# Mask set-up, weight splits, load order and identity transposes at the start of a hybrid decoder block

## The chip, the cores and the metric

The kernel runs on one core of a Trainium2 chip. The core has a matrix engine (TensorE; PE in the profile, PEld for its weight loads), a vector engine (VectorE, DVE), a scalar engine (ScalarE, ACT), a general engine (GpSimd, POOL) and a queue engine (SyncE, SP). Each takes its instructions in the order in which they are queued; they meet through semaphores. Loads and stores are DMAs, issued from the queues of SP and ACT. The metric is the device time of one execution in microseconds.

## The reference

One decoder layer over 1024 tokens of width 1024, in fp32. What matters here is how it begins and what the masks are for:

```python
h = rms_norm(x, norm1_g[l]).astype(dt)
proj = h @ w_in[l]
(hq, hf, hi, hg, sq, sk, sv, fq, fk, fv, ff) = jnp.split(proj, offsets, axis=-1)
o_hg = hgrn2_mixer(hq, hf, hi, hg, lower_bounds[l], hg_norm_g[l])   # 4 heads, chunks of 64
o_sb = stick_breaking_attn(...)    # 6 heads
o_fox = forgetting_attn(...)       # 6 heads
x = x + concat([o_hg, o_sb, o_fox]) @ w_out[l]
h2 = rms_norm(x, norm2_g[l]).astype(dt)
x = x + jnp.square(jax.nn.relu(h2 @ w_ff1[l])) @ w_ff2[l]
```

Within a chunk of 64 tokens, the HGRN2 mixer needs the products of every pair of tokens in causal order. The kernel builds them level by level, with one 0/1 mask for each level.

## The kernel before

The tokens are eight tiles of 128 (t = 0 to 7), and the width 1024 is eight slices of 128 rows of weights (k = 0 to 7). To keep fp32 accuracy, every large product is made of three matmuls (`mm3`): each operand is split into a high part (a cast to fp32r, on ACT, line 124) and a low part (operand less high part, line 127), and the products high x high, low x high and high x low are accumulated.

The work is cut into units: six attention units `m0` to `m5`, each with one stick-breaking and one forgetting head, and two HGRN2 units `hg0` and `hg1`. `ORDER` begins with m0 and hg0. For each unit the kernel loads its columns of `w_in`, splits them (`w_steps`), projects all tokens (`proj_attn`, `proj_hg`) and runs its core (`attn`, `hgrn`). The projection of the next unit lies beside the core of the present one.

The start is the first norm together with the first unit's projection:

- `load_x(t)` (line 184) loads a tile of x in two halves of 512 columns, the first from SP's queue and the second from ACT's. `load_gain` (line 174) loads the norm's gain, broadcast to all partitions, from ACT's queue.
- `norm1(t)` calls `norm_to_T`: ACT squares both halves and sums them (line 148), DVE adds the two sums (line 150), `rstd_of` makes the reciprocal root from two ACT steps and four small DVE steps (lines 131 to 140), DVE scales both halves (line 153), and PE transposes the eight 128x128 blocks (line 156, `n1tp`) into PSUM buffers of the tag "z", of which there are three. `to_hT` then makes the high part on ACT (line 163, `hTh`) and the low part on DVE (line 164, `hTl`). The buffers of the squares, which the scaled rows then take, come from the tags ("e", "r", "zs")[t % 3], two of each of the first two: tiles 1, 4 and 7 use "r".
- The first unit's weights come in four pairs of row slices, called a to d. A slice has six segments of 64 columns and six further gate columns in a DMA of their own (lines 212 and 216). The high part (`whi`) is cast on ACT; the engine of the low part (`wlo`) is given by `LO`, one letter for each unit in `ORDER`: G is GpSimd, V is VectorE.
- `LOADS` gives the order in which loads are issued and in which norms and splits are written: a digit is a token tile, g the gain, a letter a to d a pair of weight slices. Once the four pairs are there and the tile number is above 2, one step of the projection follows each norm. A projection step of a token tile (`tok`, 390 columns) is 24 matmuls at lines 167 to 169 into a buffer `pj`; four token tiles can have their `pj` open at once (`P0`).

`hg_consts` makes seven masks for the HGRN2 units, one for each of six levels and one for the diagonal. Each is set to one by DVE in a scratch tile `lmf`, cut out by POOL (`affine_select`, lines 530, 533 and 544) and cast to int32 by DVE (lines 536 and 547). It is written with time 0.98, at the end of the first unit's projection. The scratch has two buffers of its own in the pool `small`. The tag "r" is used later by the scans of the stick-breaking core (`sbr`, line 404), by `hqk` and by `hon`.

The order on the engines isn't the order of the text alone: a planner takes the instructions by their place in the text as priority, and puts on each engine whatever its own estimate of times says is ready. It also hands out the buffers of a tag, each of which is free again when all who use its previous tile are done.

At the end, the feed-forward phase lays its buffers into the space of `small`'s neighbours by a table, `PLACES`, in which a tile `pad` fills what is not used.

Of the kernel before, what the change touches and what calls it, by code (L numbers as in the profile page):

```python
# [8 lines left out]
F32 = mybir.dt.float32  # L9
# [9 lines left out]
P = 128  # L19
# [7 lines left out]
LB_FLOOR = 1e-30  # L27
NEG = -1e30
ZMAX = 40.0
C = 64  # L30
NC_ = T // C
FOXH = 6
# [7 lines left out]
    "SPAN": [(0, 0), (0, -0.1), (0, 0), (-0.1, 0.05), (-0.1, 0), (-0.1, 0), (0.15, 0), (-0.05, 0)],  # L40
    "POW": [0.7, 1.1, 1.3, 1.3, 0.9, 1.2, 1, 1.5],
    "LOADS": "01g2a3b4cd567",
    "P0": "ddttdddd",
    "HI": "AAVAAAAA",
    "LO": "GVVGVGVG",
    "HPW": [0, 50, 200, 200, 200, 200, 200, 200],
    "EV": ["VA", "AA", "AA", "AA", "AA", "VA"],
    "SKEW": [2, 2, 2, 2, 2, 2],
# [10 lines left out]
def hybrid_block(ctx, tc, x, lb_logits, norm1_g, w_in, hg_norm_g, sb_q_g, sb_k_g, fox_q_g, fox_k_g,  # L59
                 fox_f_bias, w_out, norm2_g, w_ff1, w_ff2, out):  # L60
    nc = tc.nc
    V, S, G, PE = nc.vector, nc.scalar, nc.gpsimd, nc.tensor
# [3 lines left out]
    small = ctx.enter_context(tc.tile_pool(name="small", bufs=2))  # L66
    held = {}

    def pool(name, side=None, space=None):

        kw = dict(space=space) if space else dict(side=side)
        held[name] = ExitStack()
        return held[name].enter_context(tc.tile_pool(name=name, bufs=1, reuse_waits="tile", **kw))
# [10 lines left out]
    def big(tag, name, shape=None, dt=F32):  # L84
        home = sb_a if tag == "hT" else sb_w if tag in ("w", "raw", "zs", "cb", "hb", "xt") else sb_t
        return home.tile(shape or [P, SHAPE.get(tag, 512)], dt, tag=tag, name=name, bufs=BUFS[tag])

    def pt(tag, name, n=512, dt=F32):
        return ps.tile([P, n], dt, tag="ps_" + tag, name=name, bufs=PBUFS[tag])

    xf = x[0]
# [6 lines left out]

    ident = const.tile([P, P], F32, name="ident")
    make_identity(nc, ident)  # L100
    identb = const.tile([P, P], BF16, name="identb")
    V.tensor_copy(identb, ident)
    eps_t = const.tile([P, 1], F32, name="eps_t")
# [75 lines left out]
    X0 = {}  # L179

    def load_x(t):
        X0[t] = [big("pair", "x_t") for _ in range(2)]
        for c in range(2):
            (nc.sync if c == 0 else nc.scalar).dma_start(out=X0[t][c], in_=xf[t * P:(t + 1) * P, c * 512:(c + 1) * 512])

    def norm1(t):
        norm_to_T(X0.pop(t), g1b, to_hT, t, "n1")
# [160 lines left out]
    def attn(name):  # L348
# [23 lines left out]
        def qtile(h, i):  # L372
# [14 lines left out]
            for c, w in reversed(pcs):  # L387
# [7 lines left out]
                if sbk:  # L395
# [3 lines left out]
                    zs = big("zs", "sbz")[:, :w]  # L399
                    V.tensor_scalar(out=zs, in0=z, scalar1=st["r"][i // 4][:, i % 4, 0:1], scalar2=ZMAX, op0=ALU.mult, op1=ALU.min)  # L400
                    S.activation(e, zs, AF.Exp)
# [99 lines left out]
    def hg_consts():  # L501

        lbl = const.tile([P, 2], F32, name="lbl")
        nc.sync.dma_start(out=lbl, in_=lb_logits[0].rearrange("(j p) -> p j", p=P))
        lbt = const.tile([P, 2], F32, name="lbt")
        V.tensor_tensor(out=lbt, in0=lbl, in1=lbl, op=ALU.subtract)
        S.activation(lbt, lbt, AF.Exp)
        lbr = const.tile([P, 2], F32, name="lbr")
        V.reciprocal(lbr, lbt)
        V.tensor_tensor(out=lbt, in0=lbt, in1=lbr, op=ALU.mult)  # L510
        lb = const.tile([P, 2], F32, name="lb")
        V.tensor_tensor(out=lb, in0=lbt, in1=lbt, op=ALU.subtract)
        lb1 = const.tile([P, 2], F32, name="lb1")
        V.tensor_scalar(out=lb1, in0=lb, scalar1=-1.0, scalar2=1.0, op0=ALU.mult, op1=ALU.add)
        lbc = const.tile([P, 2], F32, name="lbc")
        V.tensor_scalar(out=lbc, in0=lb, scalar1=LB_FLOOR, scalar2=None, op0=ALU.max)
        S.activation(lbc, lbc, AF.Ln)
        lbcn = const.tile([P, 2], F32, name="lbcn")
        V.tensor_scalar(out=lbcn, in0=lbc, scalar1=-1.0, scalar2=None, op0=ALU.mult)


        def level_mask(n):

            f = small.tile([P, C], F32, name="lmf", bufs=2)
            V.memset(f, 1.0)
            nb = C // (2 * n)
            for h in range(2):
                fv = f[h * HD:(h + 1) * HD].rearrange("p (b e n) -> p b e n", e=2, n=n)

                G.affine_select(out=fv, in_=fv, pattern=[[-2 * n, nb], [0, 2], [0, n]], base=0, channel_multiplier=1,  # L530
                                compare_op=ALU.is_ge, fill=0.0)

                G.affine_select(out=fv, in_=fv, pattern=[[2 * n, nb], [0, 2], [0, n]], base=n - 1, channel_multiplier=-1,
                                compare_op=ALU.is_ge, fill=0.0)
            m = const.tile([P, C // 2], I32, name=f"lm{n}")
            V.tensor_copy(m.rearrange("p (b n) -> p b n", n=n), f.rearrange("p (b e n) -> p b e n", e=2, n=n)[:, :, 1, :])
            return m

        def diag_mask():
            f = small.tile([P, C], F32, name="lmf", bufs=2)  # L540
            V.memset(f, 1.0)
            for h in range(2):
                fh = f[h * HD:(h + 1) * HD]
                G.affine_select(out=fh, in_=fh, pattern=[[-1, C]], base=0, channel_multiplier=1,
                                compare_op=ALU.is_equal, fill=0.0)
            m = const.tile([P, C], I32, name="lm0")
            V.tensor_copy(m, f)
            return m

        heads = const.tile([P, 2], F32, name="heads")  # L550
        V.memset(heads, 0.0)
        for h in range(2):
            V.memset(heads[h * HD:(h + 1) * HD, h:h + 1], 1.0)
        lmask = {n: level_mask(n) for n in N_LEVELS}
        dmask = diag_mask()
        HGC.update(heads=heads, lb1=lb1, lbc=lbc, lbcn=lbcn, lmask=lmask, dmask=dmask)

# [316 lines left out]
    for o in CFG["LOADS"]:  # L874
        if o == "g":
            g1b = load_gain(norm1_g, "g1b", "hb")
        elif o in "abcd":
            loads["abcd".index(o)]()
        else:
            load_x(int(o))  # L880
# [237 lines left out]
    for q in range(NPAIR):  # L1118
        steps[q][3]()
        if AHEAD <= q + 2 < NPAIR:  # L1120
            for f in steps[q + 2][:3]:
# [9 lines left out]
    X = {}  # L1131
    U = [None] * 4

    PLACES = {"f_m": {"xo": (16, [P, 512]), "usum": (4, [P, 512]), "t1": (2, [P, 2, 512]), "ya": (3, [P, 2, 512]), "pad": (1, [P, 136 + 2048])},
              "f_hop": {"w2f": (1, [P, 2, D]), "yf": (2, [P, 2, 512]), "fof": (4, [P, 2, 512])},
              "f_h": {"w2raw": (4, [P, 2, D]), "fop": (2, [P, 2, 512]), "pad2": (1, [P, 1024])},
              "f_a": {"w2g": (1, [P, 2, D]), "fog": (14, [P, 2, 512])}}
    homes = {}
    for name, tags in PLACES.items():
        home = pool(name, "left")  # L1140
# [25 lines left out]
    for q0 in range(0, NPAIR, GM):  # L1166
        first, last = q0 == 0, q0 + GM == NPAIR
        qps = range(q0, q0 + GM, 2)
        B, t1 = {}, {}
# [61 lines left out]
        if first:  # L1231
            load_x(1, 1)
# [6 lines left out]
        if first:  # L1239
            load_x(0, 0)  # L1240
# [40 lines left out]
    held["pb"].close()  # L1281
    for name in reversed(PLACES):
        held[name].close()
# [27 lines left out]
```

## Time and profile before

| | us |
|---|---|
| median of three runs | 1349.1 |
| lowest and highest run | 1346.22 and 1351.35 |
| the profiled execution | 1347.27 |
| its span in the profile | 1345.5 |

The profile has a page with busy times and a trace that can be asked by stage, tile, line and engine. In a timeline, a row gives the start and the length in us, the engine, the line, the operation, the tile that is written and those that are read, the shape, how many alike are merged, and in brackets the idle time ahead of it with what ended it. A row of a group gives counts and shortest, median and longest duration in ns, and when the first and the last began. "SPq" and "ACTq" are the queues in which DMAs are issued. Matmuls overlap in the pipe, so their rows are longer than the distance from one to the next. The page's clock row gives the share of the full TensorE clock that was granted.

### The profile page before, as it was taken

How to read it: one execution, taken by the hardware profiler on the slowest of the kernel's cores; microseconds unless marked ns; L12 is line 12 of the kernel's file. 1: busy time of each engine (PE TensorE's matmuls, PEld its weight loads, DVE VectorE, ACT ScalarE, POOL GpSimd, SP SyncE). 2: the span in 40 equal slices, each digit the busy share in tenths (PEclk: the TensorE clock that was granted, in tenths of full speed). 3: DMA queues.
4: the chain of work that ended last, by engine and by line, in shares of the span. 5: the costliest groups of instructions: out<-in, count | busy, mean ns of one | idle time of the engine just before them, and what ended most of it. 6: DMA issues, size and time to landing. Idle time of an engine off the chain costs nothing.

```text
span 1345.5 us, 19762 instructions
## 1 busy us (share of the span) xinstructions
PE 1283.0 (95%) x7200; PEld 1063.1 (79%) x7200; DVE 985.8 (73%) x1844; ACT 727.0 (54%) x1557; POOL 90.3 (7%) x138
## 2 busy tenths in 40 slices
PE   4999889989999999999798999999999999999998
PEld 4978789878688988767586888888887788888887
DVE  6758798766768788867579766666666897786965
ACT  5658445877878457776446454455454433333330
POOL 7000021002110130000000000000000000000000
PEclk9999999989899989999898999999999999999999
DMA  8200220301203025524443434444445972634322
GB/s 231 46 17 18 62 58 18 92 16 54 49 17 79 17 57 177 183 64 125 149 152 107 164 126 164 164 130 145 149 163 175 391 247 94 218 96 153 113 79 94
DMA packets 129737, 156.57 MB, mean 116 GB/s; under 512 B 46684, under 2 KB 73308, under 8 KB 129640
## 3 DMA queue, kind: packets, MB, share of 16 engines
q1 hardware_dynamic: 104496, 109.14, 26.8%
q10 hardware_dynamic: 25144, 46.17, 9.6%
q8 instruction: 57, 0.93, 0.3%
q14 instruction: 40, 0.33, 0.1%
HBM read 108.07 MB, written 47.21 MB: 115 GB/s over the span
## 4 chain that ended last, share of the span: by engine, by line
PE 80%; DVE 10%; ACT 4%; DMA 4%; issue 2%; SPq 0%; ACTq 0%; DVEq 0%
PE pj L167 6%; PE pj L169 6%; PE pj L168 6%; PE av L465 3%; PE atp L446 2%; PE pc L1021 2%; PE pc L1022 2%; PE pc L1023 2%; PE pd L1021 2%; PE pd L1022 2%; PE pd L1023 2%; PE pc L1202 2%; PE pc L1200 2%; PE pc L1201 2%; PE pa L1023 2%; PE pa L1021 2%
## 5 line engine op out<-in xcount | busy, mean ns | idle before, releaser
L167 PE MATMUL pj<-whi,hTh 128*128 128x384 f32 (+2 forms) x512 | 172.2, 339 | 0.0
L169 PE MATMUL pj<-whi,hTl 128*128 128x384 f32 (+2 forms) x512 | 171.9, 336 | 0.0
L168 PE MATMUL pj<-wlo,hTh 128*128 128x384 f32 (+2 forms) x512 | 170.6, 334 | 0.5 <-DVE wlo L127 0.4
L124 ACT CAST fah<-ya 128x1024 fp32r<-128x1024 f32 x56 | 58.7, 1048 | 166.8 <-PE pd L1201 50.0
L167 PEld LDWEIGHTS pj<-whi,hTh 128*128 128x128 f32 x512 | 98.7, 193 | 3.6 <-issue 1.1
L168 PEld LDWEIGHTS pj<-wlo,hTh 128*128 128x128 f32 x512 | 98.5, 192 | 3.5 <-issue 1.3
L169 PEld LDWEIGHTS pj<-whi,hTl 128*128 128x128 f32 x512 | 98.4, 192 | 2.3 <-issue 1.5
L127 DVE TENSOR_TENSOR fal<-ya,fah 128x1024 fp32r<-128x1024 f32 x56 | 68.3, 1219 | 23.2 <-ACT fah L124 23.1
L465 PE MATMUL av<-at,vst 128*64 128x256 f32 x480 | 71.3, 384 | 6.3 <-DVE at L452 3.0
L450 ACT COPY at<-atp 128x128 f32<-128x128 f32 (+3 forms) x120 | 55.5, 475 | 20.5 <-PE atp L446 19.5
L465 PEld LDWEIGHTS av<-at,vst 128*64 128x64 f32 x480 | 38.3, 144 | 33.2 <-issue 8.4
L127 DVE TENSOR_TENSOR fbl<-w2raw,fbh 128x1024 fp32r<-128x1024 f32 x48 | 58.0, 1215 | 1.6 <-ACT fbh L124 1.6
L408 ACT ACTIVATE sbz<-sbz 128x128 f32<-128x128 f32 (+3 forms) x72 | 37.7, 525 | 37.8 <-DVE sbz L407 37.2
L400 DVE TENSOR_SCALAR sbz<-z,qnr 128x128 f32<-128x128 f32 (+3 forms) x72 | 42.5, 611 | 20.6 <-PE z L394 12.9
L167 PE MATMUL po<-woh,mTh 128*128 128x512 f32 x128 | 52.1, 409 | 4.5 <-DMA mTh<-mix_m 3.6
L124 ACT CAST fbh<-w2raw 128x1024 fp32r<-128x1024 f32 x48 | 50.0, 1047 | 8.1 <-DMA w2raw<-in_w_ff_dram 5.1
L391 PE MATMUL z<-kst,qj 128*128 128x512 f32 (+3 forms) x144 | 51.3, 384 | 2.8 <-ACT qj L368 2.8
L1201 PE MATMUL pa<-fbl,fah 128*128 128x512 f32 x128 | 50.3, 395 | 1.9 <-DVE fbl L127 1.8
L1200 PE MATMUL pd<-fbh,fah 128*128 128x512 f32 x128 | 49.5, 399 | 2.3 <-ACT fbh L124 2.3
L168 PE MATMUL po<-wol,mTh 128*128 128x512 f32 x128 | 51.1, 399 | 0.0
L392 PE MATMUL z<-kst,qj 128*128 128x512 f32 (+3 forms) x144 | 49.6, 370 | 1.5 <-DVE qj L369 1.4
L169 PE MATMUL po<-woh,mTl 128*128 128x512 f32 x128 | 50.6, 398 | 0.0
(349 smaller groups left out, 3626.3 us busy)
## 6 DMA issues: line engine op xcount, KB each, us to landing
w1raw<-in_w_ff_dram SPq DMA_DIRECT2D x32, 512.0 KB, 4.6
w2raw<-in_w_ff_dram SPq DMA_DIRECT2D x16, 1024.0 KB, 7.1
ya<-yd_s SPq DMA_DIRECT2D x32, 512.0 KB, 3.6
yd_s<-y ACTq DMA_DIRECT2D x48, 256.0 KB, 4.6
ya<-yd_a SPq DMA_DIRECT2D x24, 512.0 KB, 3.7
wraw<-in_w_in_dram SPq DMA_DIRECT2D x48, 192.0 KB, 3.0
mix_m<-ot ACTq DMA_DIRECT2D x10, 512.0 KB, 3.7
wraw<-in_w_in_dram SPq DMA_DIRECT2D x16, 256.0 KB, 3.6
```

The lines of the kernel that those rows point to most:

```text
L124: S.copy(hi, raw)
L127: lo_eng.tensor_tensor(out=lo, in0=raw, in1=hi, op=ALU.subtract)
L167: PE.matmul(o, lhsT=lh, rhs=rh, start=start, stop=False)
L168: PE.matmul(o, lhsT=lh, rhs=rl, start=False, stop=False)
L169: PE.matmul(o, lhsT=ll, rhs=rh, start=False, stop=stop)
L450: S.copy(dst, tv)
L465: PE.matmul(o[h * HD:(h + 1) * HD, c0:], lhsT=st["v"][j // 4][:, j % 4, h, :], rhs=at[h][j // 4][:, j % 4, c0:], start=(j == 0), stop=(j = ...
L1021: PE.matmul(o, lhsT=wh[:, k], rhs=bh[:, k], start=start and k == 0, stop=False, **kw)
L1022: PE.matmul(o, lhsT=wh[:, k], rhs=bl[:, k], start=False, stop=False, **kw)
L1023: PE.matmul(o, lhsT=wl[:, k], rhs=bh[:, k], start=False, stop=k == 3, **kw)
L1200: PE.matmul(o, lhsT=lh[:, ts], rhs=rh, start=start and q == q0, stop=False, **kw)
L1201: PE.matmul(o, lhsT=lh[:, ts], rhs=rl, start=False, stop=False, **kw)
```

## The change

- The scratch of the masks, `lmf`, moves from `small` to the tag "r", and `pad` grows by the 512 bytes for each partition that become free there.
- The low parts of the first unit's weights are made on DVE.
- `LOADS` becomes tile 0, the gain, a, tile 1, b, tile 2, c, tile 3, d, and then tiles 4 to 7. In the text, the splits of a pair now follow each of the first four norms, and the projection's first step follows norm 4 instead of norm 5.
- Both halves of each tile of x are issued from SP's queue, but for the second half of tile 0, which stays with ACT.
- Thirty transposes of the identity matrix are put on PE ahead of all else, into one PSUM buffer of the tag "z". Nothing reads their result.

```diff
+WARM = 30
...
-    "LOADS": "01g2a3b4cd567",
+    "LOADS": "0ga1b2c3d4567",
...
-    "LO": "GVVGVGVG",
+    "LO": "VVVGVGVG",
...
     ident = const.tile([P, P], F32, name="ident")
     make_identity(nc, ident)
+
+    warm = pt("z", "warm")
+    for i in range(WARM):
+        PE.transpose(out=warm[:, :P], in_=ident, identity=ident)
...
     def load_x(t):
         X0[t] = [big("pair", "x_t") for _ in range(2)]
         for c in range(2):
-            (nc.sync if c == 0 else nc.scalar).dma_start(out=X0[t][c], in_=xf[t * P:(t + 1) * P, c * 512:(c + 1) * 512])
+            (nc.scalar if t == 0 and c else nc.sync).dma_start(out=X0[t][c], in_=xf[t * P:(t + 1) * P, c * 512:(c + 1) * 512])
...
         def level_mask(n):
-            f = small.tile([P, C], F32, name="lmf", bufs=2)
+            f = big("r", "lmf", [P, C])
...
         def diag_mask():
-            f = small.tile([P, C], F32, name="lmf", bufs=2)
+            f = big("r", "lmf", [P, C])
...
-    PLACES = {"f_m": {..., "pad": (1, [P, 136 + 2048])},
+    PLACES = {"f_m": {..., "pad": (1, [P, 136 + 2176])},
```

More of the change, by code (lines that the diff above doesn't have):

```diff
@@ L1132, in hybrid_block @@
     U = [None] * 4
-    PLACES = {"f_m": {"xo": (16, [P, 512]), "usum": (4, [P, 512]), "t1": (2, [P, 2, 512]), "ya": (3, [P, 2, 512]), "pad": (1, [P, 136 + 2048])},
+    PLACES = {"f_m": {"xo": (16, [P, 512]), "usum": (4, [P, 512]), "t1": (2, [P, 2, 512]), "ya": (3, [P, 2, 512]), "pad": (1, [P, 136 + 2176])},
               "f_hop": {"w2f": (1, [P, 2, D]), "yf": (2, [P, 2, 512]), "fof": (4, [P, 2, 512])},
```

## The prediction

> **What bounds the kernel now.** I read the page's busy shares first, then the busy time by stage, then the first 64 us as a timeline, engine by engine.
>
> ```profile
> span 1345.5 us, 19762 instructions
> ...
> PE 1283.0 (95%) x7200; PEld 1063.1 (79%) x7200; DVE 985.8 (73%) x1844; ACT 727.0 (54%) x1557; POOL 90.3 (7%) x138
> ```
> ```profile
> 0.00:14.00 14.00, 0.00 (x0) 0.00 (x0) 4.84 (x28) 7.26 (x22) 12.14 (x35) 1.00 0.92 265
> 14.00:25.00 11.00, 7.06 (x27) 6.09 (x28) 9.94 (x23) 6.38 (x20) 6.78 (x10) 0.84 0.96 238
> 25.00:40.00 15.00, 15.00 (x95) 14.85 (x94) 13.50 (x45) 10.97 (x40) 5.97 (x9) 1.00 0.90 196
> 40.00:50.00 10.00, 10.00 (x66) 9.84 (x65) 9.20 (x25) 6.30 (x20) 0.57 (x1) 1.00 0.00 1
> ```
>
> PE is the bound: of 62.5 us in which it idles, 17.9 lie before 25 us (14.0, and 11.0 less 7.06), and from 25 to 50 it never stops. (Columns of a stage: length; busy time of PE, PEld, DVE, ACT, POOL; granted clock; DMA share; GB/s.) So the change is worth what it brings the unbroken PE work forward. That work, the first unit's projection, ends here:
>
> ```profile
> 63.03 0.34 PE L167 MATMUL pj<-whi,hTh 128*128 128x390 f32 x1
> ...
> 63.39 0.34 PE L169 MATMUL pj<-whi,hTl 128*128 128x390 f32 x1
> 63.57 0.40 PE L167 MATMUL pj<-hTh,whi 128*128 128x512 f32 x1
> ```
> ```profile
> 33.11 1.03 PE L156 MATMUL n1tp<-ident,n1sq 128*128 128x128 f32 x8
> 33.90 0.43 PE L168 MATMUL pj<-wlo,hTh 128*128 128x390 f32 x1
> ```
>
> A matmul starts every 0.18 us (three from 63.03 to 63.57), a transpose takes 0.11 (just under 0.9 us from the first of eight to the next in line, with the pipe's tail). The stage holds 8 token tiles x 24 matmuls x 0.178 = 34.2 us, 64 norm transposes x 0.11 = 7.0, and 8 more for keys and gates, 0.9: 42.1 us. It ends at 63.5, so it runs as if PE had started at **21.4 us** and never stopped. What held it off is on DVE:
>
> ```profile
> 7.96 0.10 DVE L150 TENSOR_TENSOR n1s<-n1ss 128x1 f32<-128x1 f32 x1
> ...
> 10.41 0.16 DVE L138 SCALAR_TENSOR_TENSOR n1t<-n1t,n1v 128x1 f32<-128x1 f32 x1
> 11.71 0.18 DVE L536 CAST lm<-lmf 128x32 int32<-128x32 f32 x1 [1.14 <-POOL lmf L533]
> 11.80 1.82 DVE L140 SCALAR_TENSOR_TENSOR n1r<-n1t,n1y 128x1 f32<-128x1 f32 x1
> ...
> 13.68 1.43 DVE L153 SCALAR_TENSOR_TENSOR n1sq<-x_t,n1r,g1b 128x512 f32<-128x512 f32 x2
> ...
> 15.72 4.32 DVE L153 SCALAR_TENSOR_TENSOR n1sq<-x_t,n1r,g1b 128x512 f32<-128x512 f32 x4
> ...
> 20.85 0.68 DVE L164 TENSOR_TENSOR hTl<-n1tp,hTh 128x512 fp32r<-128x512 f32 x1
> ```
> ```profile
> 31.34 1.41 DVE L153 SCALAR_TENSOR_TENSOR n1sq<-x_t,n1r,g1b 128x512 f32<-128x512 f32 x2
> ```
> ```profile
> 15.76 5.29 POOL L127 TENSOR_TENSOR wlo<-wraw,whi 128x384 fp32r<-128x384 f32 x6
> ```
>
> The first norm's sum and its 0.16 us steps stand in DVE's queue behind mask casts that wait for POOL, and where POOL splits weights, DVE's own operations stretch: 4.32 us for four scalings, against 1.41 for two at 31.34, when POOL is idle.
>
> **The change part by part.** *Masks.* They now take their scratch from the two "r" buffers, which the norm squares of tiles 1, 4 and 7 use ahead of them in program order, so they come behind the last norm. Tile 0 then meets no mask:
>
> ```profile
> 4.84 0.63 ACT L148 ACTIVATE n1sq<-x_t 128x512 f32<-128x512 f32 x1 [2.75 <-DMA x_t<-in_x_dram]
> ...
> 5.47 0.61 ACT L148 ACTIVATE n1sq<-x_t 128x512 f32<-128x512 f32 x1
> ...
> 9.80 0.29 ACT L131 ACTIVATE n1ln<-n1s,eps_t 128x1 f32<-128x1 f32 x1
> 10.00 0.19 ACT L133 ACTIVATE n1y<-n1ln 128x1 f32<-128x1 f32 x1
> ```
> ```profile
> L153 DVE SCALAR_TENSOR_TENSOR n1sq<-x_t,n1r,g1b x16: 737/748/1584, 13.7 to 44.0; 128x512 f32<-128x512 f32 x16
> L174 ACTq DMA_DIRECT2D g1b<-in_norm_g_dram x2: 453/453/453, 1.7 to 2.2; - x2
> ...
> DMA to landing us min/median/max: 5.6/6.0/6.3
> ```
>
> Both squares end at 6.2; five DVE steps of 0.16 and ACT's two (0.29, 0.19) give the scale at about 7.6. The gain row g1b lands 5.6 to 6.3 us after issue at 1.7 and 2.2, so at 7.3 and 8.5: scaling 7.6 to 9.2, first transpose at **8.4** instead of 14.60. *Loads.* All but one half of x goes to SP, so ACT loses seven issues (0.33 us each; one of them waited in ACT's order until 18.85) and SP issues 31 transfers before the constants: 15 halves of x and 16 pieces of weight.
>
> ```profile
> L184 SPq DMA_DIRECT2D x_t<-in_x_dram x8: 327/403/430, 0.8 to 18.6; - x8
> L184 ACTq DMA_DIRECT2D x_t<-in_x_dram x8: 334/334/445, 0.8 to 18.8; - x8
> ```
> ```profile
> L212 SPq DMA_DIRECT2D wraw<-in_w_in_dram x14: 378/434/560, 2.2 to 30.0; - x14
> L216 SPq DMA_DIRECT2D wraw<-in_w_in_dram x8: 339/542/681, 4.2 to 16.5; - x8
> ```
>
> That is 15 x 0.40 + 8 x (0.43 + 0.54) = 13.8 us of SP, less than the about 23 us that the same bytes take on DMA engines that are 0.92 to 0.96 busy: cost 0, unless SP waits, then up to 2 us on the last tiles, which nobody wants before 30 us. The order matters: the fourth pair of weight rows now has four token tiles ahead of it, not five, so 4.1 MB instead of 4.6; at 250 GB/s and from 1 us on it lands at 17 to 18. A token can't be finished before.
>
> *Splits on DVE.* Eight of 384 columns and eight of 6:
>
> ```profile
> L127 DVE TENSOR_TENSOR wlo<-wraw,whi x32: 533/552/694, 61.1 to 430.7; 128x384 fp32r<-128x384 f32 x24, 128x512 fp32r<-128x512 f32 x8
> ```
>
> 8 x (0.55 + 0.15) = 5.6 us more on DVE, 1.4 per pair of rows. Against that it is rid, before the last norm, of seven mask casts of 0.18, of 1.6 in the stretched L140 and of 1.5 in the four scalings (4.32 against 2 x 1.41): 4.4 us, about 1 less than comes. And now splits and norms share a queue. One step (a norm and a pair) is five small operations 0.8, scaling 1.41, hTl 1.37, pair 1.4: 5.0 us. Four steps from 7.0 end at 27; pairs are split at about 10.6, 15.6, 20.6 and 25.6, and the loads, by 18 us, are ahead of that.
>
> *PE under these.* One token against one pair is 6 matmuls, 1.07 us. By 17.5 there is work for two tiles' transposes (1.75) and four such pieces (4.3). From the third split, 19.7 on, more is ready than PE can do: the third tile's transposes 0.87, two pieces for old tokens, three for the new one, then the fourth split with eight. PE has done 6.9 us by 19.7, so it runs as if started at 19.7 - 6.9 = **12.8**. Bounds: 11.0 if the splits are put ahead of the scalings (all work of 18 us then done 1.8 earlier), 15.0 if each of four steps loses 0.5 us to DVE and ACT waiting for each other. Gain 21.4 - 12.8 = **8.6 us**, between 6.4 and 10.4.
>
> *Thirty transposes.* ident is ready at 1.65, long before x. They cost PE nothing while it is idle until 8.4; at 0.23 us (below) they end at 8.6, a delay of 0.2, and much less if the clock rises in between. What they can bring is the clock:
>
> ```profile
> 21.00:22.00 1.00, 0.41 (x2) 0.42 (x3) 1.00 (x3) 0.00 (x0) 0.05 (x1) 0.64 1.04 373
> 22.00:23.00 1.00, 1.00 (x6) 1.00 (x5) 0.97 (x4) 0.27 (x1) 0.00 (x0) 0.50 1.03 369
> ...
> 24.00:25.00 1.00, 1.00 (x5) 0.96 (x5) 0.24 (x3) 1.00 (x5) 0.00 (x0) 0.66 0.05 0
> ```
> ```profile
> 14.60 1.94 PE L156 MATMUL n1tp<-ident,n1sq 128*128 128x128 f32 x8 [14.60 <-POOL lmf L533]
> ...
> 17.37 0.87 PE L156 MATMUL n1tp<-ident,n1sq 128*128 128x128 f32 x4
> 21.59 1.11 PE L156 MATMUL n1tp<-ident,n1sq 128*128 128x128 f32 x4 [3.35 <-DVE hTl L164]
> ```
>
> The granted clock falls to 0.50 at about 21.3 and is back at about 24.7, 3.4 us later. Eight transposes at 14.60 take 1.94 against 1.03 when warm: half rate at first. PE was half-rate for some 6.4 us of work, which cost 3.2 us, already inside the 21.4. After, little work is ready before 17 us, so a cold clock hides in waits: I take 0.5 of the 8.6 as owed to the thirty, bounds 0 and 3.2. A rule speaks against them: the Trainium skill, "TensorE: Matmul & The Clock Gate", Part 4, says that transposes don't count as activity and don't release the clock. The trace leans the other way: in the 3.4 us before 17.9, 2.4 us were transposes and 1.0 matmuls, and the group of four at 17.37 took 0.87, between the cold 1.11 and a warm 0.60, as if released halfway. No run here has transposes alone.
>
> *Behind the stage.* Buffers, operations and the padded plan of the last phase are the same size, so I cost them 0. The 26 mask selects (this row, as many of L533, two of L544) now run beside the last tokens:
>
> ```profile
> L530 POOL TENSOR_SCALAR_AFFINE_SELECT lmf<-lmf x12: 241/352/890, 1.8 to 10.3; 64x64 f32<-64x64 f32 x12
> ```
> ```profile
> L404 DVE TENSOR_TENSOR_SCAN sbr<-sbe,zero_t x48: 407/893/1225, 79.6 to 635.2; 128x128 f32<-128x128 f32 x12, 128x256 f32<-128x256 f32 x12, 128x384 f32<-128x384 f32 x12, 128x512 f32<-128x512 f32 x12
> ```
>
> From about 44 us (the last scaling at 44.0, less some) they need 26 x 0.35 = 9 us, at worst 26 x 0.9 = 23: over by 53 to 67. The next user of "r" is the first scan, at 79.6 now, 71 then. Cost 0.
>
> The profiled execution took 1347.27 us, 1.8 more than its span; the median of three is 1349.1. Sum: 1347.27 - 8.6 = 1338.7; on the median, which I forecast, **1340.5**.
>
> **The rivals.** *DVE becomes the bound.* From 25 to 50 us, the stretch with the later norms, the copies out of PSUM and the first half's finish, it was busy 13.50 + 9.20 = 22.7 us; less 1.2 for stretching of that kind (an estimate from the 1.5) it is through at 27 + 21.5 = 48.5. PE wants the last tile at 12.8 + 42.1 - 4.3 = 50.6. That slack of 2 us is all; DVE is 13.5 of 15 busy already. If it is slower by 5 to 6 us, 3 to 4 are lost: 1344.
>
> *The transposes don't release the clock* and PE is cold where it matters, just when the backlog forms at 19.7: up to 3.2 us lost, half of it likely: 1342. That is what the Trainium skill's rule above would lead to.
>
> *The change doesn't do what it says:* the masks, which depend on nothing, get both "r" buffers at 1 us, before tile 1 asks. Then the casts stay in front and tile 1's squares wait as well; of the gain only the scalings' 1.5 us is left, and tile 1's wait against it: 1348. Program order of the buffers speaks against it.
>
> *Given back later.* The order of all engines is planned anew from a shifted start. 44.6 us of PE idle lie behind 25 us, in many waits of 0.5 to 4 us; if these grow by a fifth, the gain is gone: 1349.
>
> *Slower.* Masks block the first scan: DVE holds casts that wait for slow selects in front of the norm and copies that free PSUM. It decides once the masks end after 71; PE has the next projection, about 40 us, as filler, so a net loss needs them 20 us late and that filler used up: 1357.
>
> **How the numbers follow.** Forecast 0.52 (1338 to 1342.3 is its core), DVE bound 0.18, cold clock 0.09, masks early 0.07, given back 0.09, slower 0.05. Half a per cent, about what a measurement tells from no change, is 6.7 us: below 1342.4 is faster. The forecast gives 0.49 of that, the cold clock 0.05, a lucky new order 0.02: 0.56. Same: 0.38. Slower: 0.06. The range leaves out the worst 0.1 above and the best below: bounds 10.4 plus some order luck give 1335; above, the given-back case, 1349.5.
>
> **What would show it.** First norm transpose at 8 to 9 us; no POOL split; mask selects behind 40; last 390-column matmul of the first unit at 54 to 56 instead of 63.4 and PE unbroken from about 20. Transposes falling from 0.23 to 0.11 us inside the thirty show that they release the clock. Wrong if PE has gaps of over 1 us behind 20, if DVE's last hTl comes after 51, or if idle time behind 60 us grows by several us.

## The result and the profile after

| | before | after |
|---|---|---|
| median | 1349.1 us | 1333.6 us |
| lowest and highest run | 1346.22 and 1351.35 | 1331.99 and 1340.04 |
| the profiled execution | 1347.27 | 1340.04 |
| its span | 1345.5 | 1338.3 |

The ratio is 0.9898, with a 95% interval from 0.9876 to 0.9919: 1.0% faster, about 14 us at the interval's middle, where 8.6 were forecast. The profiled execution happens to be the slowest of its four; two further profiles of the same program, taken later (`after_again`, `after_third`), have spans of 1333.0 and 1332.8 us. What differs between them is part of the answer. One run of the experiment masks_only below, of 5885.86 us, is left out of its ratio.

The page of after, its first lines:

```profile
span 1338.3 us, 19827 instructions
...
PE 1289.4 (96%) x7230; PEld 1067.3 (80%) x7230; DVE 984.2 (74%) x1860; ACT 727.5 (54%) x1557; POOL 79.0 (6%) x122
```

The busy time by stage of after (columns as in the prediction):

```profile
0.00:14.00 14.00, 10.62 (x50) 8.69 (x50) 7.21 (x30) 8.99 (x26) 1.51 (x10) 1.00 0.95 235
14.00:25.00 11.00, 10.35 (x63) 9.96 (x64) 9.78 (x30) 9.10 (x33) 0.00 (x0) 1.00 0.94 277
25.00:40.00 15.00, 12.84 (x81) 11.83 (x80) 12.75 (x52) 9.96 (x34) 0.40 (x1) 1.00 0.78 174
40.00:50.00 10.00, 10.00 (x66) 9.68 (x65) 7.64 (x24) 4.16 (x13) 4.59 (x14) 1.00 0.21 35
```

PE now works nearly through from 9 us on (of the 10.62 up to 14 us, 6.17 are the thirty transposes), but from 25 to 40 us, where it never stopped before, it idles for 2.16. PE's timeline of after says where:

```profile
1.68 6.17 PE L105 MATMUL warm<-ident 128*128 128x128 f32 x30 [1.68 <-POOL ident masks.py:199]
9.07 1.32 PE L161 MATMUL n1tp<-ident,n1sq 128*128 128x128 f32 x8 [1.22 <-DVE n1sq L158]
...
30.42 0.45 PE L172 MATMUL pj<-whi,hTh 128*128 128x390 f32 x1 [0.67 <-ACT hTh L168]
...
32.26 0.66 PE L161 MATMUL n1tp<-ident,n1sq 128*128 128x128 f32 x4 [1.22 <-DVE hTl L169]
...
56.79 0.34 PE L174 MATMUL pj<-whi,hTl 128*128 128x390 f32 x1
56.97 0.39 PE L172 MATMUL pj<-hTh,whi 128*128 128x512 f32 x1
```

The first norm transpose starts at 9.07 us (14.60 before), and the first unit's 390-column projection gives way to the 512-column one at 56.97 (63.57 before). I call that last moment the **end of the head**. The head is 6.6 us shorter in this profile, and 7.6 and 8.0 in the two others, where it ends at 55.97 and 55.59. The two gaps of 0.67 and 1.22 us are new. DVE's timeline of after shows what it did ahead of them:

```profile
8.27 1.42 DVE L158 SCALAR_TENSOR_TENSOR n1sq<-x_t,n1r,g1b 128x512 f32<-128x512 f32 x2
...
20.85 0.64 DVE L132 TENSOR_TENSOR wlo<-wraw,whi 128x384 fp32r<-128x384 f32 x2 [0.55 <-ACT whi L129]
...
27.96 0.15 DVE L889 TENSOR_SCALAR gq_fx<-gq_fx 128x1 f32<-128x1 f32 x1 [1.61 <-DMA gq_fx<-in_fox_q_norm_g_dram]
28.03 0.22 DVE L145 SCALAR_TENSOR_TENSOR n1r<-n1t,n1y 128x1 f32<-128x1 f32 x2
28.22 2.74 DVE L158 SCALAR_TENSOR_TENSOR n1sq<-x_t,n1r,g1b 128x512 f32<-128x512 f32 x4
31.45 0.16 DVE L511 TENSOR_TENSOR lbt<-lbl 128x2 f32<-128x2 f32 x1 [0.49 <-DMA lbl<-in_lb_logits_dram]
...
46.72 0.69 DVE L169 TENSOR_TENSOR hTl<-n1tp,hTh 128x512 fp32r<-128x512 f32 x1 [0.30 <-ACT hTh L168]
```

A scaling of 0.15 us of a small constant, the query gain `gq_fx`, stands in DVE's queue ahead of the norms of tiles 4 and 5, and waits 1.61 us for its load. These two norms then come as one lump of 2.74 us, and no copy for PE (`hTl`) gets through. SP's queue in after shows where the load is issued (start, length of the issue, what is loaded, count):

```profile
15.83 5.63 SPq L189 DMA_DIRECT2D x_t<-in_x_dram  x8
...
25.58 0.59 SPq L115 DMA_DIRECT2D gq_fx<-in_fox_q_norm_g_dram  x1
...
28.60 0.43 SPq L509 DMA_DIRECT2D lbl<-in_lb_logits_dram  x1
```

The constants stand behind x; the second half of `gq_fx` is issued at 25.58, and DVE's wait ends 2.4 us later. Their place behind x is not new. In the kernel before, the same issue and the same scaling are these:

```profile
23.55 0.59 SPq L110 DMA_DIRECT2D gq_fx<-in_fox_q_norm_g_dram  x1
```
```profile
32.74 0.14 DVE L884 TENSOR_SCALAR gq_fx<-gq_fx 128x1 f32<-128x1 f32 x1
```

There DVE asked at 32.74 and waited for nothing. In after it asks at 26.35, six us earlier, because its first norms are through sooner. That SP is late, with both halves of x in its queue, adds to it in the profiled execution alone: in the two other profiles the issue is at 23.18 and 23.90, as before, and DVE still waits, 0.47 and 0.58 us for `gq_fx` and then 0.75 and 0.63 for `lbl`. PE's idle time between 28 and 33 us is 2.16 us in the first profile, 1.30 and 0.92 in the two others. The head ends 1.0 and 1.4 us earlier in them, most of it for that reason.

The last view is that of the thirty transposes in after, up to 6.9 us and behind it (shortest, median and longest ns of one):

```profile
L105 PEld LDWEIGHTS warm<-ident x5: 230/230/230, 6.0 to 6.9; 128*128 128x128 f32 x5
...
L105 PEld LDWEIGHTS warm<-ident x5: 141/143/230, 6.9 to 7.5; 128*128 128x128 f32 x5
```

They start at half rate, 230 ns for each weight load, and end at the full one, 141 ns. Nothing but transposes had run on PE. (The clock column shows 1.00 for this stage all the same: the trace's clock record begins only with this release, at 7.2 us.)

### The profile page after: what moved, and what is told of

Its sections match the earlier page's. It is cut to its first block, busy times and chain, and to the rows that moved or that the text cites. A ratio compares the mean times of both kernels' runs of the same rounds, so it can differ in the third digit from the quotient of the medians.

```text
span 1338.3 us, 19827 instructions
## 1 busy us (share of the span) xinstructions
PE 1289.4 (96%) x7230; PEld 1067.3 (80%) x7230; DVE 984.2 (74%) x1860; ACT 727.5 (54%) x1557; POOL 79.0 (6%) x122
## 4 chain that ended last, share of the span: by engine, by line
PE 82%; DVE 8%; DMA 4%; ACT 3%; issue 1%; SPq 1%; ACTq 0%
PE pj L172 7%; PE pj L174 6%; PE pj L173 6%; PE av L470 4%; PE atp L451 3%; PE pc L1027 2%; PE pc L1026 2%; PE pc L1028 2%; PE pd L1026 2%; PE pd L1027 2%; PE pd L1028 2%; PE pc L1206 2%; PE pc L1205 2%; PE pc L1207 2%; PE pa L1026 2%; PE pa L1028 2%
## 5 line engine op out<-in xcount | busy, mean ns | idle before, releaser
L455 ACT COPY at<-atp 128x128 f32<-128x128 f32 (+3 forms) x120 | 55.9, 476 | 17.4 <-PE atp L451 14.9
```

Of the source, the lines that this page charges most:

```text
L455: S.copy(dst, tv)
```

## The experiments

All ratios are to the kernel before on the same chip, with their 95% intervals. "Head" is the end of the head in the run's profile. Line numbers are those of each kernel; in most of them the same line stands some lines further down than before, up to six.

| run | head, us | median, us | ratio |
|---|---|---|---|
| before | 63.57 | 1349.1 | |
| after | 56.97 | 1333.6 | 0.9898 (0.9876 to 0.9919) |
| after_again | 55.97 | 1334.83 | 0.9889 (0.9873 to 0.9904) |
| after_third | 55.59 | 1334.4 | 0.9894 (0.9882 to 0.9907) |
| no_warm | 56.41 | 1336.23 | 0.9901 (0.9885 to 0.9917) |
| splits_pool | 57.51 | 1338.17 | 0.9927 (0.9914 to 0.9941) |
| masks_early | 58.96 | 1336.69 | 0.9911 (0.9898 to 0.9925) |
| loads_old | 60.38 | 1343.55 | 0.9962 (0.9949 to 0.9974) |
| consts_early | 54.23 | 1339.82 | 0.9927 (0.9911 to 0.9943) |
| consts_pool | 56.56 | 1338.06 | 0.9922 (0.9908 to 0.9936) |
| consts_late | 58.64 | 1335.01 | 0.9906 (0.9892 to 0.9919) |
| masks_only | 61.24 | 1346.56 | 0.9967 (0.9950 to 0.9984) |
| warm_only | 63.55 | 1342.07 | 0.9958 (0.9946 to 0.9970) |
| warm_one | 63.79 | 1345.9 | 0.9981 (0.9972 to 0.9990) |

### The parts, one taken back at a time

**after_again and after_third**: the changed kernel itself, twice more.

> The changed kernel once more, nothing edited. In its first profile the first 512-column projection matmul (the end of the first unit's projection) started at 56.97 us, against 63.57 before: 6.6 us earlier, while the medians differ by 15.5 us. Theory 1 (the start is all that the change gains, the rest is the spread of single runs through the clock): over more runs the ratio comes to about 0.993 to 0.995, that is 7 to 9 us, and runs with a higher granted clock are the shorter ones in both kernels. Theory 2 (the newly planned order behind the start gains as well): the ratio stays at 0.990, about 13 us, the start again gives 6 to 7 us, and the milestones behind 600 us show the rest.

> The changed kernel once more, beside the two others. If the time behind the head goes with the time that PE spends at half clock (54.5 us of it with 1281.3 behind the head, and 37.5 with 1277.0, in two profiles so far), this third profile lies on the same line: a quarter of a us more behind the head for each us more of half clock. If that was chance, 1277 to 1281 without regard to it. Median 1333 to 1336.

They agree with after within their intervals: the change is worth 1.0 to 1.1%.

**no_warm**: the changed kernel without the thirty transposes, which nothing reads.

```diff
-    warm = pt("z", "warm")
-    for i in range(WARM):
-        PE.transpose(out=warm[:, :P], in_=ident, identity=ident)
```

> The changed kernel without the thirty identity transposes. Theory 1 (they release the clock and that is worth little, because PE has little to do until about 17 us): the first norm's eight transposes take about 1.9 us instead of 1.32, the first matmuls start every 0.33 us, the clock comes back after 3.4 to 6.8 us of work, and the first 512-column matmul starts at 57.0 to 58.5, so 0 to 1.5 us later. Rival (transposes don't release the clock, as the Trainium skill states): nothing of this differs, since the clock would have been released by the real matmuls in both. Rival 2 (they are worth much): 60 us or later, 3 us or more lost, the price of the half-rate stretch before.

PE's first row in this kernel:

```profile
9.42 1.94 PE L157 MATMUL n1tp<-ident,n1sq 128*128 128x128 f32 x8 [9.42 <-DVE n1sq L154]
```

The eight transposes take 1.94 us at half rate instead of 1.32, yet the head ends at 56.41, between the three profiles with the thirty (55.59 to 56.97), a little before the 57.0 to 58.5 of theory 1. In the head the thirty are worth between nothing and 0.8 us: PE waits 0.62 us for DVE at 15.33 anyway. The time is 1.4 us above that of after_again on the same chip (1336.23 against 1334.83).

**splits_pool**: the first unit's splits back on POOL.

```diff
-    "LO": "VVVGVGVG",
+    "LO": "GVVGVGVG",
```

> The changed kernel with the first unit's low parts back on POOL. Theory 1 (POOL's splits stretch DVE's scalings and come late): scalings take about 1.0 us each beside POOL's splits instead of 0.71, the fourth pair's low part ends later than the 21.3 us it has on DVE, and the first 512-column matmul starts 1 to 3 us later, at 57.5 to 60. Rival (DVE is the bound of the stage and is rid of 5.6 us): 1 to 3 us earlier, 53.5 to 56.

The groups of the first 50 us in this kernel (busy us and mean ns of one behind the first bar), and one row of PE's timeline:

```profile
L158 DVE SCALAR_TENSOR_TENSOR n1sq<-x_t,n1r,g1b 128x512 f32<-128x512 f32 x16 | 13.5, 887 | 0.2
...
L132 POOL TENSOR_TENSOR wlo<-wraw,whi 128x384 fp32r<-128x384 f32 x8 | 8.7, 1090 | 11.2 <-ACT whi L129 8.0 <-DMA x_t<-in_x_dram 3.1
```
```profile
13.63 0.44 PE L173 MATMUL pj<-wlo,hTh 128*128 128x390 f32 x1 [0.70 <-POOL wlo L132]
```

The stretching is back: 13.5 us for sixteen scalings, against 11.2 in the same view of after (748 ns each). A split takes 1090 ns on POOL (555 on DVE in after). The head loses 0.5 to 1.9 us against the three profiles of after.

**masks_early**: the masks' scratch back in `small`, so that nothing holds the masks behind the norms.

```diff
-            f = big("r", "lmf", [P, C])
+            f = small.tile([P, C], F32, name="lmf", bufs=2)
```

(The same in both places, and `pad` back to 136 + 2048.)

> The changed kernel with the masks' scratch back in two buffers of its own, all else as changed. Theory 1 (mask casts in DVE's queue ahead of the first norm are the largest part): the first norm's transpose starts at 12 to 14 us instead of 9.1 and the first 512-column matmul at 58.5 to 61 instead of 56 to 57. Rival (with the splits off POOL the selects run at their short length, 26 x 0.35 = 9 us, and are through before the norm needs DVE): 9 to 11 us and 56 to 57.5.

DVE's, PE's and the stage's row in this kernel:

```profile
12.80 0.18 DVE L541 CAST lm<-lmf 128x32 int32<-128x32 f32 x1 [1.26 <-POOL lmf L538]
```
```profile
14.23 0.45 PE L173 MATMUL pj<-wlo,hTh 128*128 128x390 f32 x1 [1.59 <-DVE wlo L132]
```
```profile
14.00:25.00 11.00, 9.32 (x39) 8.86 (x40) 9.58 (x35) 5.79 (x22) 1.31 (x3) 0.69 0.94 276
```

A cast waits for POOL on DVE, the splits behind it are late, PE waits 1.59 us for them, and then the clock falls (0.69 from 14 to 25 us). The head loses 2.0 to 3.4 us. The first norm, though, was not held up until 12 to 14 us, as theory 1 had it: its transposes start at 9.26.

**loads_old**: the old `LOADS` string, and the second halves of x again from ACT's queue.

```diff
-    "LOADS": "0ga1b2c3d4567",
+    "LOADS": "01g2a3b4cd567",
...
-            (nc.scalar if t == 0 and c else nc.sync).dma_start(out=X0[t][c], ...)
+            (nc.sync if c == 0 else nc.scalar).dma_start(out=X0[t][c], ...)
```

> The changed kernel with the loads in their old order (three tiles of x ahead of the first pair) and alternately from SP and ACT; norms and splits then follow that order in the text too. Theory 1 (the order sets when PE has two pieces to work on): the first pair's high part starts at 9 us or later instead of 6.6, the fourth pair's split ends 2 us later, PE has a gap of 2 us or more between 11 and 18 us, and the first 512-column matmul starts at 58 to 60. Rival (the engines are behind the loads anyway): 56 to 57.5.

PE's and DVE's rows in this kernel:

```profile
12.61 1.97 PE L161 MATMUL n1tp<-ident,n1sq 128*128 128x128 f32 x8 [5.12 <-DVE n1sq L158]
...
20.17 0.44 PE L172 MATMUL pj<-whi,hTh 128*128 128x390 f32 x1 [1.69 <-ACT hTh L168]
```
```profile
9.96 0.56 DVE L132 TENSOR_TENSOR wlo<-wraw,whi 128x384 fp32r<-128x384 f32 x1 [2.15 <-ACT whi L129]
```

The first weights come 3 us later (the first split at 9.96, 7.14 in after), the first norm 3.5, and later on ACT stands 2.46 us before a cast whose weights aren't there (at 19.53), with PE's `hTh` behind it. The head loses 3.4 to 4.8 us, the most of the three parts in this comparison. The run took order and queues of the loads back at once, so which of the two counts stays open.

Two of these losses come out too small. After has the new wait, and so has loads_old (DVE waits 2.57 us for `lbl`, until 30.57, and PE idles 1.34 us ahead of 35.38). Splits_pool and masks_early have not: there DVE asks for `gq_fx` only at 29.24 and 30.60, when it has landed, and PE is busy for all of 28 to 33 us. Against consts_early below, which is after without that wait and ends its head at 54.23, they lose 3.3 and 4.7 us; loads_old loses 6.2, of which 1.34 are the wait. So **the loads and the masks cost about the same when they are taken back, near 5 us each**, and the splits some 3. Half rate is a part of each: the granted clock from 14 to 19 us is 0.66, 0.67 and 0.73 in splits_pool, masks_early and loads_old, and 1.00 in after.

The parts add up to more than the 9.3 us between 63.57 and 54.23: each hides behind the others. The other side shows it too.

**masks_only**: the kernel before with the masks' move alone.

> The kernel before with one part of the change: the masks' scratch in the r buffers. Loads, load order, splits on POOL as before, no identity transposes. Theory 1 (the mask casts in DVE's queue held the first norm): the first norm transpose starts at 9 to 10 us instead of 14.60 and the first 512-column matmul at 58.5 to 61, 2.5 to 5 us earlier; the rest up to 57.0 is the splits and the order. Rival (the weights' arrival and POOL's splits held PE, not the norm): the first transpose comes early and the stage still ends at 62.5 to 63.5.

PE's first row in this kernel:

```profile
13.26 1.09 PE L156 MATMUL n1tp<-ident,n1sq 128*128 128x128 f32 x4 [13.26 <-DVE n1sq L153]
```

1.3 us earlier, not the 6 that the masks were thought to hold it. DVE's row says what holds it now:

```profile
11.18 0.77 DVE L137 TENSOR_TENSOR n1t<-n1y 128x1 f32<-128x1 f32 x1 [3.58 <-ACT n1y L133]
```

DVE waits 3.58 us for a step of the root on ACT, and ACT, in order, has the cast of the first weights ahead of it, which waits for its load until 10.34. The old order of loads thus holds the first norm nearly as long as the masks did; loads_old, where all else is as in after, gives 12.61. The head gains 2.3 us. The time gains 0.2 to 0.5%, with runs spread from 1340.46 to 1349.2 us.

### The new wait

**consts_early**: the changed kernel, with the three constants on which DVE waits loaded ahead of tile 5.

```diff
+            if o == "5":
+                gq_sb, gq_fx = col(sb_q_g, "gq_sb"), col(fox_q_g, "gq_fx")
+                lbl = const.tile([P, 2], F32, name="lbl")
+                nc.sync.dma_start(out=lbl, in_=lb_logits[0].rearrange("(j p) -> p j", p=P))
             load_x(int(o))
...
```

(The lines that loaded them further down are left out.)

> The changed kernel with the loads of gq_sb, gq_fx and lbl issued from SP's queue ahead of tile 5 instead of behind tile 7 and most other constants. In the changed kernel DVE stood 1.61 us for gq_fx and 0.49 for lbl, with two tiles' scales behind them in its queue, and PE then idled 2.2 us between 28.5 and 32.3. Theory (this wait is the new head-of-line block and is worth its length): no such wait, PE has no gap between 28 and 33, and the first 512-column matmul starts at 54.3 to 55.2, about 2 us earlier. Rival (tiles 5 to 7 come late instead, by the 2.8 us of SP's issues): it stays at 56.5 to 57.5 with a wait on x.

A stage and the end of the head in this kernel:

```profile
25.00:40.00 15.00, 15.00 (x99) 14.72 (x97) 14.44 (x54) 11.69 (x41) 0.40 (x1) 1.00 0.99 225
```
```profile
54.23 0.39 PE L172 MATMUL pj<-hTh,whi 128*128 128x512 f32 x1
```

The gap is gone, and the head ends at 54.23, 1.4 to 2.7 us earlier than in the three profiles of after. So the wait's cause is settled. **But the time is 5 us worse than after's** (after_again, on the same chip). A better head came with a worse kernel.

**consts_pool**: the constants issued from POOL's queue at the start.

```diff
-        nc.sync.dma_start(out=t[0:HD], in_=v)
+        nc.gpsimd.dma_start(out=t[0:HD], in_=v)
```

(And the other constants alike.)

> The changed kernel with the eleven small loads of constants issued by POOL instead of SP. Theory A (the head-of-line wait for gq_fx is worth its length, as the run with early constants showed: 54.23): the first 512-column matmul starts at 54 to 55, and the total is 1.5 to 2.5 us below the changed kernel's if nothing else differs. Theory B (each edit has the order behind the start planned anew, and that is worth up to 5 us either way, by the time that PE is at half clock and by waits): the head comes to 54 to 55 and the total still lies anywhere from 1329 to 1340.

The gap at 28 to 33 us is gone here too. But POOL makes the identity matrix, and that comes 1.9 us later behind the issues (the thirty start at 3.55); PE's first matmul waits 1.70 us for ACT, and the clock from 14 to 19 us is 0.66. The head ends at 56.56, not at the 54 to 55 that both theories had, and the time is 1338.06.

**consts_late**: the two scalings written behind the norms.

> The changed kernel, with the two scalings of the query gains written behind the norms instead of ahead of the last of them. Theory 1 (the 2.9 us that PE loses from 28.5 to 32.3 are a queue wait: DVE stands in order behind a scaling that waits for a small late load): the gap goes, PE is unbroken from 25 to 40 us (15.0 of 15.0), the first 512-column projection matmul starts at 53.5 to 54.5 instead of 56 to 57. The time follows only if nothing is lost behind: 1331 to 1332. Rival (the gap is DVE short of time, or ACT late with hTh): the gap stays, 56 to 57, time the same as the changed kernel's. Theory 3 (behind the head the order is planned anew and gives or takes up to 5 us, mostly as stretches of half clock): head at 54 but time anywhere from 1331 to 1340, and span less head between 1277 and 1283.

DVE's and PE's rows in this kernel:

```profile
30.24 0.16 DVE L511 TENSOR_TENSOR lbt<-lbl 128x2 f32<-128x2 f32 x1 [1.81 <-DMA lbl<-in_lb_logits_dram]
```
```profile
31.50 0.45 PE L172 MATMUL pj<-whi,hTh 128*128 128x390 f32 x1 [1.34 <-ACT hTh L168]
```

The experiment missed its aim: the planner put the scalings ahead of the norms all the same, and the next constant, `lbl`, took over the wait (1.81 us). PE idles 1.60 us between 28 and 33 us, as in the profiles of after; but it then runs at a clock of 0.76 from 33 to 40 us (1.00 in after), and the head ends at 58.64, later than after's. Yet the median, 1335.01, is as good as after's. Head and time go apart a second time.

### Behind the head

**warm_only**: the kernel before with the thirty transposes alone.

```diff
     make_identity(nc, ident)
+    warm = pt("z", "warm")
+    for i in range(WARM):
+        PE.transpose(out=warm[:, :P], in_=ident, identity=ident)
```

> The kernel before, with the thirty transposes of the identity alone. Theory 1 (the clock is not what holds the head): the first norm transpose stays at 14 to 15 us, bound by DVE, eight of them take 1.94 again since PE idles for some 6 us ahead of them or 1.0 to 1.3 if the clock lasts; the first 512-column matmul starts at 63 to 63.6; time within 0.3 % of the kernel before, 1345 to 1353. Rival (the clock was worth its bound of 3.2 us in the head): 60.3 to 61, time 1345 to 1346. If the planner takes another order behind the head, span less head lies at 1277 to 1280 instead of 1281.9.

PE's rows in this kernel's head:

```profile
1.67 6.36 PE L105 MATMUL warm<-ident 128*128 128x128 f32 x30 [1.67 <-POOL ident masks.py:199]
14.53 1.76 PE L161 MATMUL n1tp<-ident,n1sq 128*128 128x128 f32 x7 [6.49 <-DVE n1sq L158]
```

Nothing in the head moves: first norm transpose 14.53 (14.60 before), end 63.55 (63.57). Compared instruction by instruction, every engine's order is that of the kernel before, but for the thirty. And still **it is 0.42% faster**, some 6 us. Theory 1 was right on the head and wrong on the time; the rival was wrong on both. Where the time went is seen in two profiles side by side, whose spans differ by 5.6 us. First PE's rows before:

```profile
602.82 0.50 PE L167 MATMUL po<-woh,mTh 128*128 128x512 f32 x1 [2.44 <-DMA mTh<-mix_m]
...
658.88 0.50 PE L167 MATMUL po<-woh,mTh 128*128 128x512 f32 x1 [0.78 <-DVE x L859]
...
719.68 0.79 PE L1021 MATMUL pa<-b11h,w11h 128*128 128x512 f32 x1 [4.11 <-ACT w11h L124]
```

and then the same matmuls in warm_only. The row at 719.68 above is the 13th matmul of its group; the last two rows here are the first and the 13th of that group:

```profile
601.49 0.50 PE L172 MATMUL po<-woh,mTh 128*128 128x512 f32 x1 [0.49 <-DMA mTh<-mix_m]
...
656.31 0.50 PE L172 MATMUL po<-woh,mTh 128*128 128x512 f32 x1 [0.78 <-DVE x L864]
...
711.66 0.80 PE L1026 MATMUL pa<-b11h,w11h 128*128 128x512 f32 x1 [1.40 <-DVE t L980]
...
717.13 0.69 PE L1026 MATMUL pa<-b11h,w11h 128*128 128x512 f32 x1
```

At 602 us PE waits 2 us less for a transfer; by 656 us the same matmul is 2.6 us ahead. More comes around 716 us, where the feed-forward phase begins. The stage there, before:

```profile
705.00:716.00 11.00, 9.30 (x46) 6.84 (x44) 10.01 (x21) 5.76 (x14) 0.00 (x0) 1.00 0.64 210
716.00:729.00 13.00, 7.99 (x20) 5.88 (x21) 13.00 (x22) 11.13 (x22) 0.00 (x0) 0.61 0.19 61
```

and in warm_only:

```profile
705.00:716.00 11.00, 8.43 (x30) 6.22 (x30) 10.73 (x22) 6.88 (x17) 0.00 (x0) 0.76 0.55 178
716.00:729.00 13.00, 11.08 (x42) 7.47 (x41) 13.00 (x23) 11.14 (x23) 0.00 (x0) 0.94 0.11 39
```

In both the clock is halved for a while (the third number from the end). Before, PE first runs its matmuls at full rate, waits 4.11 us for ACT, and is then at half rate when the backlog is there to be done. In warm_only the half rate comes earlier, on the matmuls ahead of that wait, and fills the wait: the 13th starts at 717.13 without one. By the first matmul of `pc` (732.80 before, 728.39 there) warm_only is 4.4 us ahead. The last 1.2 of the 5.6 us are not followed here.

**warm_one**: the same with a single transpose.

> The kernel before, with a single transpose of the identity in place of the thirty that made it 6.5 us faster while the head of the kernel stayed where it was (63.55 us) and no other instruction changed its place on any engine. Theory A (the extra tile is what counts: it takes one of the three buffers of the tag z, so that all later tiles of that tag change places, or it shifts the addresses of what follows; the work of the thirty counts nothing): 1341 to 1343, as with thirty, first 512-column matmul at 63.5. Theory B (the work counts: the early release of the clock, or the time at which the engine first runs, moves later half-clock stretches to places where the engine has slack): 1347 to 1350, as the kernel before.

1345.9 us, 0.19% faster than before, with the head at 63.79: between both theories. A transpose that nothing reads and that changes no order came with 2.6 us, thirty of them with some 6. Not told apart is what does it: the transposes' work, or the buffer of the tag "z" that the extra tile takes, which both kernels have. Nor do the 6 us carry over: in the changed kernel the thirty are worth 1.4 us (no_warm against after_again).

Half rate differs as much between profiles of one program. Two stages of after:

```profile
716.00:729.00 13.00, 13.00 (x49) 10.29 (x48) 11.88 (x20) 7.71 (x15) 0.00 (x0) 0.82 0.06 21
1030.00:1065.00 35.00, 30.52 (x119) 23.89 (x118) 27.57 (x28) 18.46 (x21) 0.00 (x0) 0.90 1.01 377
```

and of after_again, the same program:

```profile
716.00:729.00 13.00, 12.70 (x54) 9.60 (x53) 12.26 (x21) 9.38 (x18) 0.00 (x0) 1.00 0.10 26
1030.00:1065.00 35.00, 31.86 (x131) 25.59 (x132) 28.38 (x29) 17.93 (x20) 0.00 (x0) 0.95 1.03 387
```

In the first stage PE does 54 matmuls at full clock against 49. The trace records the clock in windows of 3.41 us; behind the head, 16 of them are at half rate in after, 11 in after_again and 12 in after_third, and span less head is 1281.3, 1277.0 and 1277.2 us. Over all 14 profiles of this study a window more goes with some 0.8 us more behind the head (correlation 0.78; from 10 windows and 1274.7 us in consts_late to 17 and 1281.9 before). A third profile of after was expected on the line of the first two, and 1277.2 us with 12 windows is; it also lies in the range that was named for chance.

So the gain of about 14 us has two parts. **Some 7 us are the head** (6.6 to 8.0 by profile): the change's own, by mechanisms that the runs above take apart. **The other 6 to 7 us lie behind the head**, where the change adds and removes no work. In the profiles they go with which short waits of PE, around 600, 640 to 660, 705 to 729 and 1030 to 1065 us, fall together with half rate; that this is their cause is argued from profiles side by side, and no edit shows it. Median less head is 1285.5 us before, and no less in consts_early (1285.6) and masks_only (1285.3), but 1278.9 in after_again, 1278.5 in warm_only and 1276.4 in consts_late: no part of the change goes with it. What makes it lasting stays open: all runs of before lie between 1346.2 and 1353.4 us and those of warm_only between 1341.5 and 1346.0, though the mean granted clock is no better there (0.973 to 0.978, 0.975 to 0.982 before). Warm_only's profile has 14 half-rate windows behind the head and three in it; before has 17 and one, but its clock record begins only at 17.9 us. Where they fall differs; one pair of profiles shows that, but not why.

## Why the prediction came out as it did

*The bound and the way of counting* held in the head: PE stayed the bound at 96%, and the span of after's profile is 7.2 us shorter with a head shorter by 6.6.

*The first norm transpose* came at 9.07, against 8.4: half of the first pair was split ahead of the norm instead of behind it. On ACT the cast of the first slice stands ahead of the root and waits 0.93 us for its load, until 6.59; on DVE the low part of that slice, 0.64 us at 7.14, stands ahead of the scale.

*The splits* were costed too high in sequence: the last pair was split at 20.85 to 21.5, not at 25.6. The prediction chained four steps of 5.0 us, with two low-part copies in each, and the planner let splits go ahead of them. The loads bound the last pair: ACT waits 1.38 us for its second slice, until 20.30, where the sum had it landed at 17 to 18.

*The head's start.* "As if started" was forecast at 12.8. consts_early, which lacks only the new wait, gives 54.23 - 42.1 = 12.1: that step of the sum was 0.7 us from right. With the wait the three profiles give 13.5, 13.9 and 14.9. The step that failed is **SP at "cost 0, unless SP waits, then up to 2 us on the last tiles, which nobody wants before 30 us"**. SP did take longer than the 13.8 us of the sum: its issues of x and of these weights run from 0.81 to 21.46 us. But the price was not on the tiles of x. It was on the constants behind them, 0.9 to 2.2 us of PE's time, and mostly not because SP came to them later, but because DVE, ahead of its old times by the change itself, asks for them at 26 us instead of 32.7. The prediction counted SP's transfers up to the constants and stopped there, and its list of DVE's work has no scaling of a constant in it.

*The thirty*: 0.5 us was taken, between 0 and 3.2; no_warm puts them between nothing and 0.8 in the head. The Trainium skill's rule in "TensorE: Matmul & The Clock Gate", Part 4, that transposes don't engage the full clock, does not hold for these: with thirty of them alone on PE, weight loads went from 230 to 141 ns. (The trace lists them as matmuls; it doesn't show whether they use the transpose mode of which that page speaks.) The rival that hung on it is out: in after no window before 60 us is at half rate once they are done.

*The shares of the parts.* The prediction led with the masks and gave the loads' order a few lines. Alone, the masks are worth 2.3 us in the head; taken back from the change, with the new wait out of the comparison, the masks and the order and queues of the loads cost near 5 us each, and the splits some 3.

*Masks behind the stage*: costed at 0, and right. POOL's selects run from 44.33 to 58.72 us, inside the forecast 44 to 67, and the first scan isn't held.

*Behind the stage*, **"so I cost them 0"**: wrong, by 6 to 7 us, and here the forecast's size was lost. Its own given-back rival named what moved, the many short waits, with a fifth of the idle time as its price; the sign was the other one. None of its steps gives these 6 to 7 us: for the prediction they are luck. The range's lower end, 1335, allowed for a little of it; the median of 1333.6 lies 1.4 us below that end, and 0.9898 of 1349.1, 1335.3, just above.

*The other rivals.* DVE was not the bound: its last `hTl` came at 46.72, not after 51. The masks were not early. The slower case did not arise.

*What would show it*: no POOL split, masks behind 40 and the fall inside the thirty were seen. "PE unbroken from about 20" was not: the gap of 1.22 us ahead of 32.26 is over the 1 us that was named as a sign of being wrong, and it led to the new wait. The last 390-column matmul came at 56.79 (forecast 54 to 56); 55.41 in after_third.

## What to carry to other kernels

When a change brings an in-order engine forward, list all that stands in its queue, down to the scaling of a constant of a few hundred bytes, and see when the load of each is issued: what was early enough before can be too late now. Judge a change to one stage by that stage's own end, in several profiles, and not by the total alone: here an inert edit moved the total by 0.4% with the stage unchanged, and a better stage (consts_early) came with a worse total. A part that is taken back can also take back a wait that the change brought, so compare with a kernel that is free of it. Repeat the kernel before under an edit that does nothing, before a gain of half a per cent is put down to a reason.

## What the hardware showed unasked

- Transposes of the identity, alone on PE, release the clock here. After began them at 1.68 us and was at full rate from about 7.2; in after_third the same program was from about 5.2.
- All halvings and releases within a profile lie whole multiples of 3.41 us apart: in after the first three halvings are at 188.12, 276.86 and 355.37 us, 26 and 23 windows apart. The grid stands differently to the start of the program in each execution: counted back from the first release, its first point is at 0.4 us in after and 1.9 and 1.8 in the two repeats. The Trainium skill says the same in "TensorE: Matmul & The Clock Gate", Part 1: the window of 3413 ns runs free. The trace agrees. One program had 16, 11 and 12 half-rate windows behind the head in three executions, which fits a cost of short waits that depends on where they fall in the grid.
- A load of 256 bytes took 2.4 us from the start of its issue to its use in after (25.58 to 27.96), and 3.2 us in consts_late (23.67 to 26.88). SP took 0.43 to 0.60 us for an issue of this kind, once 1.51: eleven loads of constants keep its queue from 21.51 to 29.03.
